# The prelude of a one-layer attention and retention trunk: order of loads, squares and row copies

## The chip, the cores and the metric

The kernel runs on one core of a Trainium2 chip. The time is that of the device for one execution, in microseconds (us); 975.65 us is the median of three runs before the change. A profile of one further execution is the source of all rows.

## What is computed

One layer for 512 positions of width 2048. An adaptive norm turns the row vector c into a shift, a scale and a gate; the normed x goes through one input projection of 7168 columns, then windowed attention and retention, an output projection and a final norm. Only the beginning matters here:

```
mod = silu(c) @ w_ada + b_ada
shift, scale, gate = split(mod, 3)
h = rms_norm(x, g) * (1 + scale) + shift
proj = h @ w_in
```

## The kernel before

**Tiling.** x comes in four tiles of 128 positions (xt0 to xt3, in order outputs xt_110 to xt_113), each 128 by 2048. Products need h with the width on the partitions, so each tile is squared, divided by its root mean square and turned by PE in blocks of 128 columns. The width is cut into 16 blocks k; block 0 is treated apart, so that products with it can start while the other columns of w_ada are still coming. The blocks are grouped as 1, 2, 2, 3, 4, 4.

**The prelude, written out by hand from `warm(WARM[0], psk3)` on.** `squares_a(t)` squares the lower half of a tile on ACT (tile sqa) and `squares(t)` the upper half on DVE (sqd); `factor(t)` makes the factor rsx from both sums, on DVE and then with a power on POOL. `scaled(t, a, b)` multiplies columns a to b by it on DVE. `k0_part(t)` turns block 0 of the tile on PE into psk, or into psk3 for tile 3, and `turned(t, b)` turns one of four groups of further blocks into a PSUM bank psx, which `evacuated(t, b, act)` copies to xT on ACT. The bank comes from a pool of four.

`sums0(b, i)` multiplies one half i of the first shift (b = 0) or scale columns (b = 1) of w_ada, tile raw0, by silu(c) on PE: eight products each, into psa. `sums0_turned()` copies the resulting row on ACT (tile row0) and turns it on PE; `shift_scale0()` adds the small rows and gives sv and av on DVE. The small rows are b_ada and norm_gain, loaded as bg_row, turned on PE and copied as bg on DVE (`turn_rows`). With sv and av, `h0_high` makes the high part of h block 0 (hh0) on ACT, `h0_sum` and `h0_low` the low part (hl0) on DVE; each once for tiles 0 to 2 (A) and once for tile 3 (B). Every product of the projections is made of three with high and low parts (mm3, lines 89 and 91).

`warm(n, ps)` are n products of constants, whose result nobody reads.

**Behind the prelude.** For the next blocks of width, w_ada is loaded in pieces (araw, three buffers). The first piece is multiplied by silu(c) on ACT (line 206), the others are added on DVE (line 210, aacc); the first of them for blocks 1 and 2 is kept behind the last hh0. Its sums go through PE to sv and av, and from there to hh1, hh2 (line 165). Beside it w_in is loaded (raw), split into high (whi, ACT, line 544) and low (wlo, DVE, line 545) and multiplied.

**Order.** Steps inside `pin` keep their order in the program; the others (the ada pieces, the conversions and products, the last scaling of tile 3's upper half) are put among them by a scheduler. Each engine then runs its list strictly in turn, and SP issues its loads strictly in turn too. Loads are issued on three queues: SP's (q1), ACT's (q10) and POOL's (q0). Before the change xt0 is split between ACT and SP, xt1 is on POOL, xt2 and xt3 on ACT, and raw0's four quarters on SP; w_in and araw follow on SP.

The lines that the prediction names: 116 raw0's loads, 123 x's loads, 199 araw's, 565 w_in's; 268 to 270 the small rows; 292 sums0; 299 the row copy; 301 its turn; 304 to 306 shift and scale; 311 and 316 squares; 321 and 325 factor; 329 and 451 scalings; 335 and 343 turns; 354 copies; 364 and 367 h0; 374 warm products. The changed kernel has the same steps one to seven lines away: its sums0 is line 295, its first ada step line 207.

Of the kernel before, what the change touches and what calls it, by code (L numbers as in the profile page):

```python
# [17 lines left out]
P = 128  # L18
D = 2048
S = 512  # L20
# [16 lines left out]
N_PERSIST = 2  # L37
ADA_SPAN = 0.65
TAB_SPAN = 16
WARM = 9, 2, 8, 6, 4  # L40
LAG = 3
RAW, RAW1, WB, LOOK, LEAD, LEAD1, EB, YB = 3, 3, 3, 2, 4, 8, 1, 22
GR = 2
# [6 lines left out]
def trunk_kernel(ctx, tc, x, c, norm_gain, w_ada, b_ada, w_in, w_out, dec_f, dec_b, final_gain, out):  # L50
    nc = tc.nc
    x2, o2 = x[0], out[0]
# [9 lines left out]
    def bank(pool, nm):  # L62
        return pool.tile([P, 512], F32, tag="b", name=nm)
# [49 lines left out]
    xn = [(x3p if t == 3 else xp).tile([P, D], F32, name=f"xt{t}") for t in range(NT)]  # L113

    def load0(q, b, i):
        q.dma_start(
            raw0[b][:, i * 8 : (i + 1) * 8],
            wa[i * 8 * P : (i + 1) * 8 * P, b * D : b * D + P].rearrange("(a p) f -> p a f", p=P),
        )

    nc.gpsimd.dma_start(c_row, c.rearrange("b (k p) -> (b k) p", p=P))
    for q, t, a, b in ((nc.scalar, 0, 0, 1024), (nc.sync, 0, 1024, D), (nc.gpsimd, 1, 0, D), (nc.scalar, 2, 0, D), (nc.scalar, 3, 0, D)):
        q.dma_start(xn[t][:, a:b], x2[t * P : (t + 1) * P, a:b])
    for i in range(2):
        for b in range(2):
            load0(nc.sync, b, i)
    ssx = const.tile([P, NT, 2], F32, name="ssx")
    rsx = const.tile([P, NT], F32, name="rsx")

# [20 lines left out]
    pin = tc.keep_in_program_order  # L150
# [114 lines left out]
    bg = const.tile([P, 48], F32, name="bg")  # L265

    def turn_rows():
        pin(nc.tensor.transpose(ps0[:, 64:112], bg_row, ident[0:48, 0:48]))
        nc.vector.tensor_copy(bg, ps0[:, 64:112])
        nc.vector.tensor_scalar_add(bg[:, 16:32], bg[:, 16:32], 1.0)  # L270

    def silu_c_pe():
        pin(nc.tensor.transpose(ps0[:, 0:NK], c_row, ident[0:NK, 0:NK]))
# [1 line left out]
    def silu_c():  # L275
        pin(nc.scalar.activation(ce, ps0[:, 0:NK], AF.Exp, scale=-1.0))
        pin(nc.vector.tensor_scalar_add(ce, ce, 1.0))
        pin(nc.vector.reciprocal(ce, ce))
        pin(nc.vector.tensor_tensor(ct, ps0[:, 0:NK], ce, op=ALU.mult))
# [3 lines left out]
    ps0 = bank(psA, "ps0")  # L283
# [5 lines left out]
    def sums0(b, i):  # L289
        for a in range(8 * i, 8 * i + 8):  # L290
            pin(
                nc.tensor.matmul(
                    psa[0:1, b * P : (b + 1) * P], ct[:, a : a + 1], raw0[b][:, a, :],
                    start=a + b == 0, stop=a == NK - 1, skip_group_check=True,
                )
            )

    def sums0_turned():
        pin(nc.scalar.copy(row0, psa[0:1, 0 : 2 * P]))
        for b in range(2):  # L300
            pin(nc.tensor.transpose(psa[:, 256 + b : 257 + b], row0[:, b * P : (b + 1) * P], ident[0:1, 0:1]))

    def shift_scale0():
        pin(nc.vector.tensor_tensor(sv[:, 0:1], psa[:, 256:257], bg[:, 0:1], op=ALU.add))
        pin(nc.vector.tensor_tensor(av[:, 0:1], psa[:, 257:258], bg[:, NK : NK + 1], op=ALU.add))
        pin(nc.vector.tensor_tensor(av[:, 0:1], av[:, 0:1], bg[:, 32:33], op=ALU.mult))


    def squares_a(t):
        sa = xp.tile([P, 1024], F32, tag="sqa", name="sqa")  # L310
        marks["sq"] = pin(nc.scalar.activation(sa, xn[t][:, 0:1024], AF.Square, accum_out=ssx[:, t, 0:1]))

    def squares(t):
        sd = aap.tile([P, 1024], F32, tag="aacc", name="sqd")
        v = xn[t][:, 1024:2048]
        pin(nc.vector.tensor_tensor_reduce(sd, v, v, 1.0 / D, EPS, ALU.mult, ALU.add, ssx[:, t, 1:2]))

    def factor(t):
        ms = small.tile([P, 1], F32, tag="ms1", name="ms1", bufs=2)
        pin(  # L320
            nc.vector.scalar_tensor_tensor(
                ms, ssx[:, t, 0:1], 1.0 / D, ssx[:, t, 1:2], op0=ALU.mult, op1=ALU.add
            )
        )
        nc.gpsimd.tensor_tensor(rsx[:, t : t + 1], ms, mhalf[:, 0:1], op=ALU.pow)

    def scaled(t, a, b):
        v = xn[t][:, a:b]
        marks["sc"] = pin(nc.vector.tensor_scalar_mul(v, v, rsx[:, t : t + 1]))
# [3 lines left out]
    def k0_part(t):  # L333
        o = psk3[:, 0:P] if t == 3 else psk[:, t * P : (t + 1) * P]
        pin(nc.tensor.transpose(o, xn[t][:, 0:P], ident))
# [3 lines left out]
    def turned(t, b, late=False):  # L339
        ps = psx[t, b] = bank(psM if late else psP, "psx")  # L340
        for k in range(*BANKS[b]):
            j = k - BANKS[b][0]
            ins = nc.tensor.transpose(ps[:, j * P : (j + 1) * P], xn[t][:, k * P : (k + 1) * P], ident)
            if not late:
                pin(ins)

    def evacuated(t, b, eng, late=False):
        k0, k1 = BANKS[b]
        for i, g in enumerate(groups):
            lo, hi = max(g[0], k0), min(g[-1] + 1, k1)  # L350
            if i and lo < hi:
                dst = xt_tiles[i][:, lo - g[0] : hi - g[0], t * P : (t + 1) * P]
                src = psx[t, b][:, (lo - k0) * P : (hi - k0) * P].rearrange("p (k f) -> p k f", k=hi - lo)
                marks[eng] = eng(dst, src)
                if not late:
                    pin(marks[eng])

    act, dve = nc.scalar.copy, nc.vector.tensor_copy
# [4 lines left out]
    def h0_high(cols, src):  # L363
        marks["hh"] = pin(nc.scalar.activation(hh[0][:, cols], src, AF.Identity, scale=av[:, 0:1], bias=sv[:, 0:1]))

    def h0_sum(cols, src):
        pin(nc.vector.tensor_scalar(tmp0[:, cols], src, av[:, 0:1], sv[:, 0:1], op0=ALU.mult, op1=ALU.add))

    def h0_low(cols):
        marks["hl"] = pin(nc.vector.tensor_tensor(hl[0][:, cols], tmp0[:, cols], f32(hh[0][:, cols]), op=ALU.subtract))  # L370

    def warm(n, ps):
        for _ in range(n):
            pin(nc.tensor.matmul(ps[:, 128:256], ones, ident, start=True, stop=True))

    A, B = slice(0, 3 * P), slice(3 * P, S)
    warm(WARM[0], psk3)
    squares_a(0)
# [5 lines left out]
    silu_c()  # L384
    warm(WARM[1], psk3)
    k0_part(0)
# [2 lines left out]
    scaled(0, 1024, D)  # L389
    turned(0, 2)  # L390
    turned(0, 3)
    for b in range(4):
        evacuated(0, b, act)
    warm(WARM[2], psk3)
    sums0(0, 0)
    turn_rows()
    squares_a(1)
    squares(1)
    factor(1)
    scaled(1, 0, P)  # L400
    scaled(1, P, 1024)
    k0_part(1)
    turned(1, 0)
    turned(1, 1)
    evacuated(1, 0, act)
    evacuated(1, 1, act)
    sums0(1, 0)
    scaled(1, 1024, D)
    turned(1, 2)
    turned(1, 3)  # L410
    sums0(0, 1)
    squares_a(2)
    squares(2)
    factor(2)
    evacuated(1, 2, act)
    evacuated(1, 3, act)
    sums0(1, 1)
    scaled(2, 0, P)
    scaled(2, P, 1024)
    sums0_turned()  # L420
    k0_part(2)
    turned(2, 0)
    turned(2, 1)
    shift_scale0()
    squares_a(3)
    squares(3)
    factor(3)
    h0_sum(A, psk[:, A])
    scaled(3, 0, P)
    scaled(2, 1024, D)  # L430
    evacuated(2, 0, act)
    evacuated(2, 1, act)
    h0_high(A, psk[:, A])
    turned(2, 2)
    warm(WARM[3], ps0)
    k0_part(3)
    warm(WARM[4], ps0)
    h0_low(A)
    marks["conv1"] = [marks["hh"], marks["hl"]]
    h0_high(B, psk3[:, 0:P])  # L440
    h0_sum(B, psk3[:, 0:P])
    h0_low(B)
    turned(2, 3)
    evacuated(2, 2, act)
    evacuated(2, 3, act)
    scaled(3, P, 1024)

    def last_rows(b):
# [868 lines left out]
```

## Time and profile before

| what | value |
|---|---|
| median of three runs | 975.65 us (975.62 to 977.54) |
| profiled execution | 977.17 us |
| its span, first to last instruction | 975.4 us |
| mean granted clock of TensorE | 0.994 |
| first raw0 sums on PE | 15.47 us |
| row copy of the raw0 sums | 29.96 us |
| first ada step (line 206) | 38.90 us |
| first product with h0 | 39.12 us |

The last four are starts, in us from the beginning of the span. PE is TensorE's products, PEld its weight loads, DVE VectorE, ACT ScalarE, POOL GpSimd, SP SyncE. In the timeline a row merges several instructions of one kind (x16), and each fp32 product of 128 columns appears as two. The 1.8 us between span and time lie outside of the instructions.

### The profile page before, as it was taken

The page shows a single profiled execution, that of the slowest core. Times are in us where ns is not written, and L with a number is a line of the kernel's source. Part 1 is how long each engine was busy: PE and PEld are TensorE (multiplying, and loading weights), DVE is VectorE, ACT ScalarE, POOL GpSimd, SP SyncE. Part 2 cuts the span into 40 slices and gives each one's busy share as a digit, 9 for nine tenths or more (in the row PEclk, how much of TensorE's full clock was granted, in tenths as well). Part 3 has the DMA queues.
Part 4 walks back from the last instruction along what each step waited for, and adds up shares of the span by engine and source line. Part 5 has one row for each costly group of instructions (what it writes and reads, how often), then busy time and mean ns, then how long its engine had stood idle before and what let it go on. Part 6 is the DMA issues. An engine that isn't in the chain of part 4 may idle for free.

```text
span 975.4 us, 14424 instructions
## 1 busy us (share of the span) xinstructions
PE 948.7 (97%) x5624; PEld 824.8 (85%) x5624; DVE 614.0 (63%) x1076; ACT 376.3 (39%) x738; POOL 12.8 (1%) x26
## 2 busy tenths in 40 slices
PE   6899899999999999999999999999999999999996
PEld 4787688887988888988998899998899988888896
DVE  3699999957868776664555456745534382535444
ACT  3654425234236554444343232422333372333321
POOL 1000000000000000000000000000000000000001
PEclk9999999999999999999999999999999999999998
DMA  9697879633652122212224625426413148234304
GB/s 330 207 313 241 284 267 314 208 102 111 187 179 80 53 85 65 66 44 87 70 84 149 197 66 184 141 80 202 123 57 95 54 169 283 87 119 140 109 1 173
DMA packets 108947, 141.49 MB, mean 145 GB/s; under 512 B 5656, under 2 KB 78024, under 8 KB 108496
## 3 DMA queue, kind: packets, MB, share of 16 engines
q1 hardware_dynamic: 107056, 134.78, 43.0%
q10 hardware_dynamic: 1584, 4.72, 1.2%
q8 instruction: 44, 0.72, 0.3%
q0 software_dynamic: 240, 1.08, 0.3%
q14 instruction: 23, 0.19, 0.1%
HBM read 136.36 MB, written 4.20 MB: 144 GB/s over the span
## 4 chain that ended last, share of the span: by engine, by line
PE 82%; DVE 7%; DMA 7%; issue 2%; ACT 1%; POOL 0%; SPq 0%; POOLq 0%; DVEq 0%; ACTq 0%
PE pp L91 24%; PE po L91 12%; PE pp L89 12%; PE pw L91 12%; PE po L89 6%; PE pw L89 6%; PE op L91 3%; DMA araw<-in_w_ada_dram 3%; DMA graw<-in_w_ada_dram 2%; PE sp L91 2%; DVE aacc L210 2%; PE op L89 2%; DMA raw<-in_w_ada_dram 1%; PE tp L776 1%; DVE acc L948 1%
## 5 line engine op out<-in xcount | busy, mean ns | idle before, releaser
L544 ACT CAST whi<-raw 128x512 fp32r<-128x512 f32 (+1 forms) x289 | 175.2, 607 | 431.8 <-PE pp L91 197.4
L545 DVE TENSOR_TENSOR wlo<-raw,whi 128x512 fp32r<-128x512 f32 (+1 forms) x289 | 193.6, 671 | 208.5 <-ACT whi L544 204.3
L91 PE MATMUL pp<-wlo,hh 128*128 128x256 f32 x576 | 161.9, 281 | 0.9 <-DVE wlo L545 0.9
L89 PE MATMUL pp<-whi,hh 128*128 128x256 f32 x576 | 162.4, 282 | 0.0
L91 PE MATMUL pp<-whi,hl 128*128 128x256 f32 x576 | 161.5, 280 | 0.0
L89 PEld LDWEIGHTS pp<-whi,hh 128*128 128x128 f32 x576 | 108.5, 188 | 2.5 <-ACT sc L845 1.7
L91 PEld LDWEIGHTS pp<-wlo,hh 128*128 128x128 f32 x576 | 108.5, 188 | 2.1 <-DVE wlo L545 1.3
L91 PEld LDWEIGHTS pp<-whi,hl 128*128 128x128 f32 x576 | 108.5, 188 | 0.0
L89 PE MATMUL pw<-hh,whi 128*128 128x512 f32 x256 | 102.4, 401 | 2.7 <-DVE acc L948 2.0
L89 PE MATMUL pp<-hh,whi 128*128 128x512 f32 x256 | 101.8, 398 | 0.4 <-DVE kl L676 0.4
L91 PE MATMUL pp<-hh,wlo 128*128 128x512 f32 x256 | 101.3, 397 | 0.7 <-DVE wlo L545 0.7
L91 PE MATMUL pw<-hh,wlo 128*128 128x512 f32 x256 | 101.6, 397 | 0.1
L91 PE MATMUL pp<-hl,whi 128*128 128x512 f32 x256 | 101.1, 395 | 0.0
L91 PE MATMUL pw<-hl,whi 128*128 128x512 f32 x256 | 101.0, 395 | 0.0
L91 PE MATMUL po<-wlo,yh 128*128 128x512 f32 (+1 forms) x252 | 92.6, 367 | 0.0
L91 PE MATMUL po<-whi,yl 128*128 128x512 f32 (+1 forms) x252 | 92.5, 367 | 0.0
L89 PE MATMUL po<-whi,yh 128*128 128x512 f32 (+1 forms) x252 | 92.5, 367 | 0.0
L210 DVE SCALAR_TENSOR_TENSOR aacc<-araw,ct,aacc 128x512 f32<-128x512 f32 (+2 forms) x75 | 75.9, 1012 | 7.0 <-ACT aacc L206 3.7
L948 DVE TENSOR_TENSOR acc<-acc,pw 128x512 f32<-128x512 f32 x100 | 66.9, 680 | 8.0 <-PE pw L91 7.6
L1001 DVE SCALAR_TENSOR_TENSOR gacc<-graw,ct,gacc 128x512 f32<-128x512 f32 x60 | 45.0, 749 | 40.2 <-DMA graw<-in_w_ada_dram 39.8
L89 PEld LDWEIGHTS pw<-hh,whi 128*128 128x128 f32 x256 | 48.1, 188 | 17.5 <-DVE acc L948 4.5
L89 PEld LDWEIGHTS pp<-hh,whi 128*128 128x128 f32 x256 | 48.1, 188 | 13.7 <-ACT e L721 0.9
(234 smaller groups left out, 1567.4 us busy)
## 6 DMA issues: line engine op xcount, KB each, us to landing
raw<-in_w_in_dram SPq DMA_DIRECT2D x94, 512.0 KB, 3.6
araw<-in_w_ada_dram SPq DMA_DIRECT2D x48, 512.0 KB, 6.1
graw<-in_w_ada_dram SPq DMA_DIRECT2D x64, 256.0 KB, 2.9
raw<-in_w_out_dram SPq DMA_DIRECT2D x32, 512.0 KB, 3.7
raw<-in_w_in_dram SPq DMA_DIRECT2D x16, 384.0 KB, 3.6
araw<-in_w_ada_dram SPq DMA_DIRECT2D x16, 384.0 KB, 5.2
res<-in_x_dram SPq DMA_DIRECT2D x16, 256.0 KB, 6.2
raw<-in_w_in_dram SPq DMA_DIRECT2D x11, 256.0 KB, 2.8
```

The costliest lines, as they stand in the source:

```text
L89: nc.tensor.matmul(o, lh, rh, start=start, stop=False, skip_group_check=True)
L91: nc.tensor.matmul(o, a, b, start=False, stop=stop and b is (rl if swap else rh), skip_group_check=True)
L210: ins = nc.vector.scalar_tensor_tensor(acc[:, :, :n], rv[:, a], ct[:, kr + a : kr + a + 1], acc[:, :, :n], op0=ALU.mult, op1=ALU.add,)
L544: c1 = nc.scalar.copy(dh, src)
L545: c2 = nc.vector.tensor_tensor(dl, src, f32(dh), op=ALU.subtract)
L776: nc.tensor.transpose(tp_[:, j * P : (j + 1) * P], pt[:, j * P : (j + 1) * P], ident)
L948: nc.vector.tensor_tensor(accs[u][i], accs[u][i], ps[i], op=ALU.add)
L1001: nc.vector.scalar_tensor_tensor(st["acc"], raw, ct[:, kr : kr + 1], st["acc"], op0=ALU.mult, op1=ALU.add)
```

## The change

Loads: xt1 and xt2 go on ACT's queue, xt3 on SP's queue behind the four raw0 quarters; POOL no longer loads x. Squares and factors of tiles 1 and 2 both come before either tile is scaled. The held-back halves of both (`turned(t, 2)`, `turned(t, 3)`) are turned behind the row's turn. `turn_rows` now only turns the rows on PE, ahead of the first sums0; their copy on DVE is the new `rows()`, put behind the scalings of tiles 1 and 2. Tile 3's squares stand ahead of the row copy and of shift and scale. The warm products go from 9, 2, 8, 6, 4 to 9, 2, 4, 4. No arithmetic is changed.

```diff
-WARM = 9, 2, 8, 6, 4
+WARM = 9, 2, 4, 4
...
-    for q, t, a, b in ((nc.scalar, 0, 0, 1024), (nc.sync, 0, 1024, D), (nc.gpsimd, 1, 0, D), (nc.scalar, 2, 0, D), (nc.scalar, 3, 0, D)):
+    for q, t, a, b in ((nc.scalar, 0, 0, 1024), (nc.sync, 0, 1024, D), (nc.scalar, 1, 0, D), (nc.scalar, 2, 0, D)):
...
             load0(nc.sync, b, i)
+    nc.sync.dma_start(xn[3], x2[3 * P : S, :])
...
-        nc.vector.tensor_copy(bg, ps0[:, 64:112])
-        nc.vector.tensor_scalar_add(bg[:, 16:32], bg[:, 16:32], 1.0)
+
+    def rows():
+        pin(nc.vector.tensor_copy(bg, ps0[:, 64:112]))
+        pin(nc.vector.tensor_scalar_add(bg[:, 16:32], bg[:, 16:32], 1.0))
...
+    evacuated(0, 0, act)
+    evacuated(0, 1, act)
+    for t in (1, 2):
+        squares_a(t)
+        squares(t)
+        factor(t)
     warm(WARM[2], psk3)
+    turn_rows()
     sums0(0, 0)
+    evacuated(0, 2, act)
+    evacuated(0, 3, act)
+    for t in (1, 2):
+        scaled(t, 0, P)
+        scaled(t, P, 1024)
+        k0_part(t)
+        turned(t, 0)
+        turned(t, 1)
+        evacuated(t, 0, act)
+        evacuated(t, 1, act)
+        sums0(t % 2, t // 2)
+    sums0(1, 1)
     scaled(1, 1024, D)
+    scaled(2, 1024, D)
+    rows()
     squares_a(3)
     squares(3)
     factor(3)
+    sums0_turned()
+    shift_scale0()
+    for t in (1, 2):
+        turned(t, 2)
+        turned(t, 3)
+    scaled(3, 0, P)
     h0_sum(A, psk[:, A])
     h0_high(A, psk[:, A])
+    k0_part(3)
     warm(WARM[3], ps0)
```

How the engines' lists change is shown at three places. First DVE, from the last scaling of tile 0 to the scale: before the change (xt_111 is tile 1, xt_112 tile 2, xt_113 tile 3; the short rows of the sums are ssx, ms the mean square):

```order
L269 COPY bg<-ps_147 128x48
L270 TENSOR_SCALAR bg<-bg 128x16
L316 ISA sqd,ssx<-xt_111 128x1024
L316 ISA ssx 128x1
L321 SCALAR_TENSOR_TENSOR ms_226<-ssx 128x1
L329 TENSOR_SCALAR xt_111<-xt_111,rsx 128x128
L329 TENSOR_SCALAR xt_111<-xt_111,rsx 128x896
L329 TENSOR_SCALAR xt_111<-xt_111,rsx 128x1024
L316 ISA sqd,ssx<-xt_112 128x1024
L316 ISA ssx 128x1
L321 SCALAR_TENSOR_TENSOR ms_275<-ssx 128x1
```

There the copy of the small rows leads, and tile 2 is squared behind tile 1's scalings. On the same engine after the change, from tile 1's upper half to shift and scale:

```order
L332 TENSOR_SCALAR xt_111<-xt_111,rsx 128x1024
L332 TENSOR_SCALAR xt_112<-xt_112,rsx 128x1024
L272 COPY bg<-ps_147 128x48
L273 TENSOR_SCALAR bg<-bg 128x16
L319 ISA sqd,ssx<-xt_113 128x1024
L319 ISA ssx 128x1
L324 SCALAR_TENSOR_TENSOR ms_292<-ssx 128x1
L445 TENSOR_SCALAR xt_113<-xt_113,rsx 128x1024
L307 TENSOR_TENSOR sv<-psa,bg 128x1
L308 TENSOR_TENSOR av<-psa,bg 128x1
L309 TENSOR_TENSOR av<-av,bg 128x1
```

The squares of tiles 1 and 2 have moved ahead of this piece, the copy of the rows stands behind the last scaling, and the scaling of tile 3's upper half, which the scheduler places, stands ahead of shift and scale; before the change it stood behind the first wlo.

Second ACT, from the row copy to the first ada step, before the change (psk holds block 0 of tiles 0 to 2, psk_148 that of tile 3):

```order
L299 COPY row_149<-psa 1x256
L311 ACTIVATE sqa,ssx<-xt_113 128x1024
L354 COPY xT_93<-psx 128x2x128
L354 COPY xT_94<-psx 128x2x128
L354 COPY xT_95<-psx 128x3x128
L364 ACTIVATE hh_77<-psk,sv,av 128x384
L544 CAST whi<-raw 128x512
L364 ACTIVATE hh_77<-psk_148,sv,av 128x128
L354 COPY xT_96<-psx 128x4x128
L206 ACTIVATE aacc<-araw,ct 128x2x256
```

And the same stretch of ACT after it:

```order
L314 ACTIVATE sqa,ssx<-xt_113 128x1024
L302 COPY row_149<-psa 1x256
L367 ACTIVATE hh_77<-psk,sv,av 128x384
L538 CAST whi<-raw 128x512
L367 ACTIVATE hh_77<-psk_148,sv,av 128x128
L357 COPY xT_96<-psx 128x4x128
L357 COPY xT_97<-psx 128x4x128
L357 COPY xT_96<-psx 128x4x128
L357 COPY xT_97<-psx 128x4x128
L207 ACTIVATE aacc<-araw,ct 128x2x256
```

Tile 3's squares now lead the row copy, and four copies instead of one stand between the last hh and the ada step.

Third PE, from the warm products behind tile 0 to the row's turn, before the change (raw_108 holds the shift columns, raw_109 the scale columns):

```order
L374 MATMUL psk_148<-ident,ones 128x128 x8
L292 MATMUL psa<-raw_108,ct 1x128 x8
L268 MATMUL ps_147<-ident,bg_row 128x48
L335 MATMUL psk<-ident,xt_111 128x128
L343 MATMUL psx<-ident,xt_111 128x128 x7
L292 MATMUL psa<-raw_109,ct 1x128 x8
L343 MATMUL psx<-ident,xt_111 128x128 x8
L292 MATMUL psa<-raw_108,ct 1x128 x8
L292 MATMUL psa<-raw_109,ct 1x128 x8
L301 MATMUL psa<-ident,row_149 128x1 x2
```

And PE's same stretch after it, with the turns that now follow:

```order
L377 MATMUL psk_148<-ident,ones 128x128 x4
L269 MATMUL ps_147<-ident,bg_row 128x48
L295 MATMUL psa<-raw_108,ct 1x128 x8
L338 MATMUL psk<-ident,xt_111 128x128
L346 MATMUL psx<-ident,xt_111 128x128 x7
L295 MATMUL psa<-raw_109,ct 1x128 x8
L338 MATMUL psk<-ident,xt_112 128x128
L346 MATMUL psx<-ident,xt_112 128x128 x7
L295 MATMUL psa<-raw_108,ct 1x128 x8
L295 MATMUL psa<-raw_109,ct 1x128 x8
L304 MATMUL psa<-ident,row_149 128x1 x2
L346 MATMUL psx<-ident,xt_111 128x128 x8
```

The turn of the small rows now leads the first sums, tile 2's first seven blocks stand between the sums, and the second half of tile 1 (and of tile 2 behind it) has moved behind the row's turn.

Further on, at the ada step of the next group but one, ACT has the step ahead of all four short sums (junk) instead of between two and two; from there on the three lists of ACT, DVE and SP soon are the same as before.

More of the change, by code (lines that the diff above doesn't have):

```diff
@@ L391, in trunk_kernel @@
     turned(0, 3)
-    for b in range(4):
-        evacuated(0, b, act)
+    evacuated(0, 0, act)
[4 more added lines that the diff above has]
+        factor(t)
     warm(WARM[2], psk3)
+    turn_rows()
     sums0(0, 0)
[L396 to L407, printed above, removed]
-    scaled(1, 1024, D)
[L409 to L424, printed above, removed]
+    evacuated(0, 2, act)
[10 more added lines that the diff above has]
+    sums0(1, 1)
+    scaled(1, 1024, D)
+    scaled(2, 1024, D)
+    rows()
     squares_a(3)
@@ L427, in trunk_kernel @@
     factor(3)
+    sums0_turned()
[4 more added lines that the diff above has]
+    scaled(3, 0, P)
     h0_sum(A, psk[:, A])
[L429 to L432, printed above, removed]
     h0_high(A, psk[:, A])
-    turned(2, 2)
+    k0_part(3)
     warm(WARM[3], ps0)
-    k0_part(3)
-    warm(WARM[4], ps0)
     h0_low(A)
@@ L442, in trunk_kernel @@
     h0_low(B)
-    turned(2, 3)
-    evacuated(2, 2, act)
-    evacuated(2, 3, act)
+    for t in (1, 2):
+        evacuated(t, 2, act)
+        evacuated(t, 3, act)
     scaled(3, P, 1024)
```

## The prediction

> **What bounds the kernel now.** The page's first part comes first: who is busy over the whole span.
>
> ```profile
> PE 948.7 (97%) x5624; PEld 824.8 (85%) x5624; DVE 614.0 (63%) x1076; ACT 376.3 (39%) x738; POOL 12.8 (1%) x26
> ```
>
> 97% is a mean over stages, and says nothing of the prelude. Next the chain of work in order of time (start, duration, what); three of its longest pieces are transfers:
>
> ```profile
> 1.19 14.23 DMA raw<-in_w_ada_dram
> ...
> 69.52 7.67 DMA araw<-in_w_ada_dram
> ...
> 158.44 6.46 DMA araw<-in_w_ada_dram
> ```
>
> So the end hangs on loads from the first microsecond on, and on araw loads as late as 158. Then the timeline of the prelude (start, duration, engine, line, operation, in brackets the idle time before it with its releaser):
>
> ```profile
> 15.47 1.91 PE L292 MATMUL psa<-raw,ct 128*1 128x128 f32 x16 [2.35 <-DMA raw<-in_w_ada_dram]
> 17.60 0.21 DVE L269 COPY bg<-ps 128x48 f32<-128x48 f32 x1 [7.42 <-PE ps L268]
> 17.93 1.22 DVE L316 CUSTOM_DVE_ANT_0 sqd<-xt 128x1024 f32<-128x1024 f32 x1
> ...
> 19.50 0.55 POOL L325 TENSOR_TENSOR rsx<-ms,mhalf 128x1 f32<-128x1 f32 x1 [11.47 <-DVE ms L321]
> ...
> 25.24 1.10 PE L343 MATMUL psx<-ident,xt 128*128 128x128 f32 x8
> 26.27 3.65 PE L292 MATMUL psa<-raw,ct 128*1 128x128 f32 x32
> 29.96 0.36 ACT L299 COPY row<-psa 1x256 f32<-1x256 f32 x1 [2.95 <-PE psa L292]
> 30.76 0.16 DVE L304 TENSOR_TENSOR sv<-psa,bg 128x1 f32<-128x1 f32 x1 [4.62 <-PE psa L301]
> 33.21 0.67 ACT L364 ACTIVATE hh<-psk,sv,av 128x384 fp32r<-128x384 f32 x1 [0.79 <-DVE ht L367]
> 33.78 0.61 ACT L544 CAST whi<-raw 128x512 fp32r<-128x512 f32 x1
> 38.08 0.46 ACT L364 ACTIVATE hh<-psk,sv,av 128x128 fp32r<-128x128 f32 x1 [3.69 <-PE psk L335]
> 38.43 0.58 ACT L354 COPY xT<-psx 128x512 f32<-128x512 f32 x1
> 38.90 0.73 ACT L206 ACTIVATE aacc<-araw,ct 128x512 f32<-128x512 f32 x1
> 39.12 0.48 PE L89 MATMUL pw<-hh,whi 128*128 128x512 f32 x1
> ```
>
> The reader is to see one serial line. The first w_ada columns (raw0) land at 15.4. Only behind their sums does PE turn bg_row; DVE, which has stood at the bg copy for 7.42 us, then squares tile 1, though the tile had been there (ACT squared its half at 12.61, below). Then come factor, scaling and transposes, tile after tile; the first ada piece (L206) starts at 38.90 and the first product with h0 at 39.12. The same windows show what the DMA engines do (the last two columns: DMA share, GB/s) and the granted clock (the column before them):
>
> ```profile
> 5.00:14.20 9.20, 7.29 (x49) 6.34 (x48) 3.45 (x9) 4.59 (x10) 0.56 (x1) 1.00 1.03 400
> 14.20:20.50 6.30, 2.16 (x18) 1.47 (x18) 2.09 (x7) 0.00 (x0) 0.55 (x1) 1.00 1.20 298
> 20.50:24.30 3.80, 3.44 (x17) 2.38 (x18) 2.27 (x4) 2.06 (x5) 0.00 (x0) 0.55 1.04 390
> 24.30:34.00 9.70, 6.92 (x60) 5.08 (x57) 4.07 (x12) 4.42 (x12) 1.10 (x2) 1.00 1.02 326
> 34.00:44.00 10.00, 9.66 (x52) 8.79 (x53) 7.25 (x14) 6.31 (x15) 0.00 (x0) 0.83 0.14 40
> 44.00:62.00 18.00, 17.26 (x101) 14.45 (x100) 16.84 (x32) 13.39 (x26) 0.00 (x0) 1.00 0.96 315
> ```
>
> The DMA engines are full to 34, idle for 86% of the next 10 us (8.6 us), full again from 44. So whatever starts the ada pieces earlier finds the engines free. Up to the araw load of 158.44 the chain alternates between DVE, such loads and PE; each load is issued when DVE frees its buffer, so an earlier start is passed on.
>
> **Part 1: the loads.** x's tile 1 leaves POOL for ACT's queue, tile 3 goes from ACT to SP's queue behind raw0. DMA queues in the window from 6 to 14 us (packets, MB, share):
>
> ```profile
> q10 hardware_dynamic: 263, 1.90, 58.7%
> q0 software_dynamic: 228, 1.08, 33.1%
> q1 hardware_dynamic: 422, 0.22, 9.2%
> ```
>
> q10 is ACT's, q0 POOL's, q1 SP's. SP's raw0 rows are 512 bytes, those of x 8 KB; packets go out at comparable counts, so raw0 gets 0.22 of 3.2 MB and moves at its own pace (298 GB/s) only when x is through. Three tiles of x stand before it now, two after the change: 1.05 MB at 400 GB/s is 2.6 us. First raw0 quarter usable: 15.47 - 2.6 = **12.85**; each further quarter (0.524 MB at 298) 1.76 later, the fourth at 18.1. x's tile 3 follows: 18.1 + 2.6 = 20.7. All this is estimated from these rows. The bytes before the w_in loads are the same, so those loads start where they did.
>
> ```profile
> 1.19 14.10 SPq L116 DMA_DIRECT2D raw<-in_w_ada_dram  x4
> 15.33 4.11 SPq L565 DMA_DIRECT2D raw<-in_w_in_dram  x6
> ...
> 1.93 0.56 POOL L123 DMA_DIRECT2D xt<-in_x_dram  x1
> ```
>
> SP's sequencer stands in raw0's issues until 15.3; these end earlier as raw0 drains earlier, and the added issue (0.46, half of the 0.92 for two at 46.69 below) stands in front of transfers that cannot move before 20.7: nothing. POOL loses an issue of 0.56; the warm-up products start that much earlier and then wait for c_row: nothing.
>
> [...]
>
> **Part 2: the squares ahead.** Durations of the moved steps:
>
> ```profile
> 12.61 1.06 ACT L311 ACTIVATE sqa<-xt 128x1024 f32<-128x1024 f32 x1 [0.60 <-DMA xt<-in_x_dram]
> ...
> 35.18 0.75 DVE L451 TENSOR_SCALAR xt<-xt,rsx 128x1024 f32<-128x1024 f32 x1
> ...
> 11.17 1.95 PE L374 MATMUL psk<-ident,ones 128*128 128x128 f32 x16
> ```
>
> ACT: two copies of tile 0 to 10.7, squares of tile 1 to 12.0, of tile 2 to 13.2 (1.06 each, with the short read of the sum behind it 1.25). DVE squares in step (1.22 each), POOL's powers take 0.55; tile 1 is scaled from about 13.6, tile 2 to 15.4. All of it lies beside the wait for raw0, which PE needs to 12.85 + 1.83 = 14.7 in any case. The two late copies of tile 0 (1.1 us of ACT) lie there too. If the cover goes (x later by 1 us), the margin of 1 us is used up and each further us costs one.
>
> PE then has no wait left: four sums of 3.65 / 2 = 1.83 are 7.3, two tiles' k0 part and seven transposes 2 x 1.10 = 2.2; 12.85 + 9.5 = 22.35, against 29.92 now. The second and fourth quarters of raw0 are there when PE arrives (14.6 for 15.8, 18.1 for 20.5).
>
> **Part 3: rows late, tile 3, h0.** The bg copy (0.21 and 0.17) now lies in DVE's free time at 17: nothing. The row copy on ACT has tile 3's squares ahead of it: 20.7 + 1.25 = 22.0, so it still starts at 22.4; by the rows 29.96 and 30.76 the shift can start 0.80 later, 23.2. On DVE tile 3's squares, factor and, as the order shows, the 0.75 us scaling of its upper half stand ahead: 22.0 + 0.2 + 0.75 (power with its gaps) + 0.75 = 23.7. That is late next. Shift and scale, three small steps of 0.16, end at 24.1, high h0 and the cast take ACT to 25.4. PE's 16 held-back transposes end at 23.2 + 2.2 = 25.4, tile 3's k0 part at 25.7, four warm products (0.98) at **26.7**, where the first product starts: 12.4 before 39.12. ACT: high part of tile 3 to 26.2, then four copies (now one) of 0.58 less some overlap to 28.4, then L206.
> Its load: w_in 1.70 MB (3328 columns of 128 rows, 4 bytes) at 390 from 20.7 is 25.1, one araw pair 1.05 MB at 326 is 28.3, landing perhaps 0.7 later. I take **28.7**, 10.2 before 38.90 (between 9.9 and 10.5). DVE is full in 44:62 (16.84 of 18), so this, not PE's 12.4, is what counts.
>
> **Part 4: what comes through.**
>
> ```profile
> 46.69 0.92 SPq L199 DMA_DIRECT2D araw<-in_w_ada_dram  x2
> ...
> 54.09 0.72 ACT L206 ACTIVATE aacc<-araw,ct 128x512 f32<-128x512 f32 x1 [1.02 <-DMA araw<-in_w_ada_dram]
> ...
> 74.64 0.28 ACT L243 ACTIVATE junk<-psm 128x128 f32<-128x128 f32 x1 [1.07 <-PE psm L238]
> ...
> 77.28 0.94 ACT L206 ACTIVATE aacc<-araw,ct 128x768 f32<-128x768 f32 x1 [2.01 <-DMA araw<-in_w_ada_dram]
> ```
>
> The load that ends a wait at 54.0 has, counted from 34, 3.14 MB to go (two w_in loads of 0.26, araw 1.05, w_in 0.52, its own 1.05): 9.6 us at 326 is 43.6, landing 44.3, a shift of 9.7 instead of 10.2. At 74.6 two sums (0.6 us) are now behind the ada piece that waits for its load: up to -0.6, and as one of DVE's casts stands one add earlier there (0.75), the load may come sooner: between -0.6 and +0.7; I take 0, the middle. From about 125 on the three orders are the same, so nothing more is gained or lost. Sum: **9.7 us**; 977.17 of the profiled execution becomes 967.5. That execution is 1.5 over the median of the runs; on the median: 975.65 - 9.7 = 966.0.
>
> **Rivals.**
> Raw0 not earlier: if raw0 gets its pace no sooner, PE starts at 15.47, all moves by 2.6, gain 7.1: 968.6. For it: SP's queue also carries tile 3. Against it: 298 GB/s begins only where x ends.
>
> A throttled clock. These rows show it:
>
> ```profile
> 20.90:24.30 3.40, 3.18 (x16) 2.31 (x17) 1.87 (x4) 2.06 (x5) 0.00 (x0) 0.53 1.03 389
> 34.55:38.00 3.45, 3.45 (x19) 3.45 (x19) 1.38 (x3) 0.00 (x0) 0.00 (x0) 0.54 0.25 77
> ```
>
> Each follows a stretch in which PE had little. With 10 warm products fewer, the 16 held-back transposes could run at half clock: 2.2 us more, gain 7.5: 968.2. Against it: PE is busy without a gap from 12.85.
> [...]
>
> The stream caps it: if the loads of 44:62 are bound by bytes throughout, the gain is the 8.6 us of idle DMA: 967.1.
>
> PE's own 12.4 comes through where araw waits shrink: 963.3.
>
> Slower: tile 3's load. ACT's row copy and DVE's shift stand behind its squares. If SP's queue did not keep its order and tile 3 landed with the last of the batch, at 34, the row copy would start at 35.25, L206 6.0 later (28.4 - 22.4) at 41.25, 2.35 behind now: 978.0. It decides from a landing at 31.65 on, and is measurable from 33.6. Against it: the rate goes from 298 to 390 at 20.5, so w_in followed raw0 in order.
>
> It does nothing: all comes back in the waits at 54 and 77, if the araw buffers and not the start set them: about 975.6. Against it: 8.6 us of idle DMA and an issue (46.69) that waits for DVE.
>
> **How the numbers follow.** Forecast 966.0, 0.62; PE's gain 0.07; cap 0.07; raw0 not earlier 0.09; clock 0.06; nothing 0.04; slower 0.05. Without the last two cases all lie between 963.3 and 968.6; raw0 and clock together would give 970.8. Range 963.2 to 969.6. Faster by over 0.2% (about what a measurement of this kernel can tell from no change, 1.95 us) 0.91, within 0.04, slower 0.05.
>
> **What would show it.** Right: first L295 at 12.9, the row copy at 22.4, L207 between 28 and 29.3, first product near 26.7, no half clock after 13, DMA share near 1 from 5 to 45, the second L207 near 44.4. Wrong: row copy later than 24 (tile 3 or raw0), a clock of 0.5 between 20 and 30, or a wait for araw at 44 to 70 that is longer than 2 us, which would give the gain back.

## The result, and the profile after

| | before | after |
|---|---|---|
| median of four runs each | 975.69 us (975.62 to 977.54) | 965.07 us (963.96 to 966.97) |
| profiled execution (its span) | 977.17 us (975.4) | 963.96 us (962.1) |
| mean granted clock of TensorE | 0.994 | 0.998 |

The ratio is 0.9889, with a 95% interval from 0.9867 to 0.9911: a gain of 10.8 us (8.7 to 13.0); between the medians it is 10.6. The forecast was 966.0 and its range 963.2 to 969.6. The first part of the page of after hardly differs from that of before:

```profile
PE 945.0 (98%) x5604; PEld 822.1 (85%) x5604; DVE 614.4 (64%) x1076; ACT 376.0 (39%) x738; POOL 13.6 (1%) x25
```

TensorE has 3.7 us less to do, and 20 products fewer in the record: the ten warm products that were dropped, each shown as two. What the change did is seen in the prelude. This is the timeline of after (start, duration, engine, line, operation, in brackets the idle time before it with its releaser):

```profile
13.38 1.91 PE L295 MATMUL psa<-raw,ct 128*1 128x128 f32 x16
...
13.98 3.16 DVE L332 TENSOR_SCALAR xt<-xt,rsx 128x128 f32<-128x128 f32 x6 [0.17 <-POOL rsx L328]
...
17.06 0.20 DVE L272 COPY bg<-ps 128x48 f32<-128x48 f32 x1
...
19.10 3.65 PE L295 MATMUL psa<-raw,ct 128*1 128x128 f32 x32
22.36 1.23 DVE L319 CUSTOM_DVE_ANT_0 sqd<-xt 128x1024 f32<-128x1024 f32 x1 [4.89 <-DMA xt<-in_x_dram]
...
23.48 0.34 ACT L302 COPY row<-psa 1x256 f32<-1x256 f32 x1
...
25.19 0.15 DVE L307 TENSOR_TENSOR sv<-psa,bg 128x1 f32<-128x1 f32 x1
...
27.50 0.46 ACT L367 ACTIVATE hh<-psk,sv,av 128x128 fp32r<-128x128 f32 x1
...
27.85 2.04 ACT L357 COPY xT<-psx 128x512 f32<-128x512 f32 x4
28.01 0.73 PE L89 MATMUL pw<-hh,whi 128*128 128x512 f32 x2 [0.94 <-ACT hh L367]
...
29.75 0.76 ACT L207 ACTIVATE aacc<-araw,ct 128x512 f32<-128x512 f32 x1
```

The serial line that could be read in the profile of before is gone. VectorE scales tile 1 at 13.98, while PE takes its first sums; the copy of the small rows (17.06) comes without a wait in front of it, where it had 7.42 us; PE runs to the last sums at 19.10 without a stop of more than 0.3. One long wait is left on DVE, 4.89 us before 22.36, and it ends on a transfer: x's tile 3. The first ada step is at 29.75, 9.15 earlier than before. The windows of after (busy time of PE, PEld, DVE, ACT, POOL, then granted clock, DMA share, GB/s) answer to those of before:

```profile
14.20:20.50 6.30, 6.30 (x55) 4.68 (x54) 3.16 (x8) 2.21 (x7) 0.70 (x1) 1.00 1.13 349
20.50:24.30 3.80, 2.69 (x25) 1.93 (x23) 1.39 (x3) 1.40 (x3) 0.36 (x1) 1.00 1.03 387
24.30:34.00 9.70, 7.87 (x47) 6.12 (x46) 7.66 (x17) 7.58 (x17) 0.19 (x1) 1.00 1.08 346
34.00:44.00 10.00, 10.00 (x56) 8.56 (x55) 9.56 (x16) 9.72 (x21) 0.00 (x0) 1.00 1.01 324
44.00:62.00 18.00, 17.92 (x116) 15.80 (x115) 16.98 (x31) 7.51 (x13) 0.00 (x0) 1.00 0.98 326
```

The stretch 34 to 44, in which the DMA engines had a share of 0.14, now has 1.01; PE's 2.16 of 6.30 us (14.2 to 20.5) have become 6.30; and the granted clock is 1.00 in each row, where it was 0.55 and 0.83 in two. The ada steps further on, in the timeline of ACT:

```profile
44.37 0.72 ACT L207 ACTIVATE aacc<-araw,ct 128x512 f32<-128x512 f32 x1 [0.18 <-DMA araw<-in_w_ada_dram]
...
65.76 0.93 ACT L207 ACTIVATE aacc<-araw,ct 128x768 f32<-128x768 f32 x1
```

They were at 54.09 and 77.28, so the shift is 9.72 and then 11.52. At the fourth and fifth it is 11.47 (112.33 to 100.86) and 10.34 (154.94 to 144.60).

### The profile page after: what moved, and what is told of

Read it like the earlier page. It is cut to its first block, busy times and chain, and to the rows that moved or that the text cites. A ratio compares the mean times of both kernels' runs of the same rounds, so it can differ in the third digit from the quotient of the medians.

```text
span 962.1 us, 14387 instructions
## 1 busy us (share of the span) xinstructions
PE 945.0 (98%) x5604; PEld 822.1 (85%) x5604; DVE 614.4 (64%) x1076; ACT 376.0 (39%) x738; POOL 13.6 (1%) x25
## 4 chain that ended last, share of the span: by engine, by line
PE 87%; DVE 5%; DMA 4%; issue 2%; SPq 1%; ACT 1%; POOL 0%; POOLq 0%; DVEq 0%; ACTq 0%
PE pp L91 24%; PE pw L91 14%; PE pp L89 12%; PE po L91 12%; PE pw L89 7%; PE po L89 6%; PE op L91 3%; PE sp L91 2%; DMA graw<-in_w_ada_dram 2%; PE op L89 2%; PE tp L770 1%; DVE aacc L211 1%; SPq L116 1%; PE sp L89 1%; DMA xt<-in_x_dram 1%
```

## The experiments

Ten runs followed; e0 is the changed kernel once more. "Gain" is one minus the ratio to the kernel before, times the median of that kernel measured beside it (975.98 for e1 to e4, 976.6 for e0, e6, e9 and e10, 976.79 for e12 and e13), with the 95% interval. The three ada steps are starts on ACT in one profiled execution each; between the changed kernel and e0 they differ by 0.2 to 0.7, less than the whole time scatters, and so they place what a kernel's time alone leaves open.

| kernel | ada steps at | median | gain |
|---|---|---|---|
| before | 38.90, 54.09, 77.28 | 975.69 | |
| after | 29.75, 44.37, 65.76 | 965.07 | 10.8 (8.7 to 13.0) |
| e0, after again | 29.91, 44.60, 66.48 | 965.47 | 11.0 (9.4 to 12.7) |
| e1, before + new loads | 36.52, 52.01, 74.14 | 974.58 | 2.3 (1.1 to 3.5) |
| e2, after - new loads | 30.45, 45.25, 66.89 | 967.41 | 9.3 (7.7 to 10.8) |
| e3, after, rows early | 34.24, 49.00, 71.47 | 970.5 | 6.1 (4.7 to 7.5) |
| e9, e3 + warm products | 33.27, 48.47, 69.33 | 968.75 | 7.8 (6.2 to 9.6) |
| e4, after, squares in turn | 29.39, 44.12, 65.60 | 964.92 | 11.0 (9.4 to 12.8) |
| e10, before + 18 and 18 warm | 39.03, 55.00, 77.29 | 975.66 | 0.8 (-0.4 to 1.9) |
| e13, before + 9 and 10 warm | 35.84, 51.46, 74.32 | 973.61 | 3.6 (2.3 to 4.9) |
| e6, after, tile 3 earlier | 29.48, 44.29, 65.70 | 965.97 | 10.8 (9.2 to 12.5) |
| e12, e6 + araw earlier | 28.38, 44.22, 65.05 | 965.23 | 12.0 (10.5 to 13.6) |

### The loads: e1 and e2

e1 is the kernel before with the change's three lines on the loads (x's tile 1 on ACT's queue, tile 3 behind raw0) and nothing else; e2 is the changed kernel without them:

```diff
-    for q, t, a, b in ((nc.scalar, 0, 0, 1024), (nc.sync, 0, 1024, D), (nc.scalar, 1, 0, D), (nc.scalar, 2, 0, D)):
+    for q, t, a, b in ((nc.scalar, 0, 0, 1024), (nc.sync, 0, 1024, D), (nc.gpsimd, 1, 0, D), (nc.scalar, 2, 0, D), (nc.scalar, 3, 0, D)):
...
-    nc.sync.dma_start(xn[3], x2[3 * P : S, :])
```

> The kernel before with the new placement of the loads alone (tiles 1 and 2 of x on ACT's queue, tile 3 on SP's behind raw0); the order of all engines stays that of before. My theory: raw0's first quarter is usable at 12.9 instead of 15.47 and everything behind it moves by that much, gain 2.6, about 973.1 us; the row copy near 27.4. Rival, the loads are the whole effect: a gain of 8 or more, below 968. Rival, the order is the whole effect: 975.7.

> The changed kernel with the old placement of the loads (tile 1 on POOL's queue, tiles 2 and 3 on ACT's); the order of all engines stays that of the changed kernel. Theory of tile 3: in the changed kernel PE reached raw0 at 13.38 and the shift waited for tile 3 (usable at 22.4), so the loads bought only part of their 2.6 us; here PE starts at 15.4, the row copy comes at 24.9 instead of 23.48, the shift at 25.7 instead of 25.19, and the loss is 0.5 to 1.2 us: 965.6 to 966.3. Rival of the prediction: the loss is the full 2.6, about 967.7. Rival, the loads are the whole effect: above 973.

From the timeline of e1:

```profile
12.98 1.91 PE L293 MATMUL psa<-raw,ct 128*1 128x128 f32 x16
...
36.52 0.73 ACT L207 ACTIVATE aacc<-araw,ct 128x512 f32<-128x512 f32 x1
```

And from that of e2:

```profile
15.67 1.91 PE L294 MATMUL psa<-raw,ct 128*1 128x128 f32 x16 [1.01 <-DMA raw<-in_w_ada_dram]
...
25.89 0.16 DVE L306 TENSOR_TENSOR sv<-psa,bg 128x1 f32<-128x1 f32 x1 [1.03 <-PE psa L303]
...
30.45 0.77 ACT L206 ACTIVATE aacc<-araw,ct 128x512 f32<-128x512 f32 x1
```

In the old order the first sums come 2.49 earlier (15.47 to 12.98) and the first ada step 2.38 earlier: the loads are worth what the first term of the prediction said, as long as everything hangs on raw0. In the new order the sums come 2.3 later without the new loads, but the first ada step only 0.70 and the second 0.88: tile 3, which comes with the rest of x there, keeps nobody waiting (shift waits for PE), and most of the 2.3 is made good behind it. On the time e2 missed: it is 2.3 above the changed kernel, over the 0.5 to 1.2 that were expected and near the rival's full 2.6. But its ada steps do not show that rival: the third is 1.13 later and the fifth 0.28 (144.88 for 144.60). The intervals of the two gains overlap, so the rest is not shown to come from the loads, and where it arises is open.

### The early rows, and the clock behind them: e3 and e9

e3 puts the small rows' turn and copy back ahead of the squares, as before the change; e9 is e3 with 24 warm products in the hole that this leaves on PE:

```diff
+    warm(WARM[2], psk3)
+    sums0(0, 0)
+    turn_rows()
+    rows()
     for t in (1, 2):
         squares_a(t)
         squares(t)
         factor(t)
-    warm(WARM[2], psk3)
-    turn_rows()
-    sums0(0, 0)
...
-    rows()
```

```diff
     turn_rows()
+    warm(24, psk3)
     rows()
```

> The changed kernel with the small rows turned behind the first sums and copied on DVE ahead of the squares of tile 1, as before the change; the rest as changed. My theory: DVE stands at the copy until the first raw0 sums are done (15.6), squares both tiles only then, tile 1's first block is turned at about 19.2 instead of 15.2, the row copy comes at about 26.7 instead of 23.48; loss 2.4 to 3.1 us, 967.5 to 968.2. Rival, the copy is hidden wherever it stands: 965.1.

> The kernel with the small rows early (e3) and 24 more products of constants on PE behind the turn of the rows, where PE stood idle for 3.78 us and the granted clock then was 0.5 from 17 to 24. Theory of the clock: of e3's loss of 5.4 us, 2.0 to 2.4 are the half clock (sums of 3.17 instead of 1.91, turns of 1.73 instead of 0.93); with PE kept busy the row copy comes at 26.7 instead of 28.87 and the time is 2 to 2.4 below e3's, about 968.2. Rival, the whole loss is DVE's wait: no change against e3, 970.5.

The timeline of e3:

```profile
14.96 0.21 DVE L272 COPY bg<-ps 128x48 f32<-128x48 f32 x1 [4.92 <-PE ps L269]
...
19.39 1.73 PE L346 MATMUL psx<-ident,xt 128*128 128x128 f32 x7 [0.21 <-DVE xt L332]
...
21.05 3.17 PE L295 MATMUL psa<-raw,ct 128*1 128x128 f32 x16
...
34.24 0.77 ACT L207 ACTIVATE aacc<-araw,ct 128x512 f32<-128x512 f32 x1
```

Its windows (busy PE, granted clock, DMA share, GB/s):

```profile
12.00:17.10 5.10, 2.18 (x18) 0.98 1.21 290
17.10:23.90 6.80, 4.98 (x23) 0.52 1.04 395
```

And the timeline of e9:

```profile
14.92 5.62 PE L377 MATMUL psk<-ident,ones 128*128 128x128 f32 x48
...
20.49 0.93 PE L346 MATMUL psx<-ident,xt 128*128 128x128 f32 x7
21.35 1.91 PE L295 MATMUL psa<-raw,ct 128*1 128x128 f32 x16
...
33.27 0.76 ACT L207 ACTIVATE aacc<-araw,ct 128x512 f32<-128x512 f32 x1
```

With the rows early, VectorE stands 4.92 us at their copy again, with the squares of two tiles behind it, and the first ada step comes 4.49 later than in the changed kernel; the time is about 5 us longer (5.4 between the medians, 4.7 between the gains), where 2.4 to 3.1 had been expected. Most of the difference is the clock. PE has 2.18 us of work in 5.1, and in the next 6.8 us the granted clock is 0.52: the seven turns take 1.73 instead of 0.93, the sums 3.17 instead of 1.91, 2.06 us for these two rows. e9 keeps the stall (4.99) and takes away the half clock. Its warm products ran to 20.4, past the 18.71 at which tile 1's block began in e3, so that the turns start 1.10 later (20.49 for 19.39); still the row copy (27.90 for 28.87) and the first ada step are 0.97 earlier than in e3. That is under half of the 2.2 expected for the row copy. The gain is 1.7 larger, where 2 to 2.4 had been expected, and the intervals overlap: it is the rows that show the effect, not the time alone. So the early rows cost twice: by the stall itself, and by the clock that falls behind PE's idle time.

### What the clock cost the kernel before: e10 and e13

Both fill the two idle stretches of PE in the kernel before with warm products, and move nothing else; e10 has 18 in each, e13 9 and 10:

```diff
     turn_rows()
+    warm(9, psk3)
     squares_a(1)
...
     h0_high(A, psk[:, A])
+    warm(10, psk3)
     turned(2, 2)
```

> The kernel before with 18 more products of constants in each of PE's two idle stretches (17.6 to 20.4 and 31.7 to 34.3), behind which the granted clock was 0.5 for 3.4 us each; nothing else moves. Theory of the clock: the first half-clock stretch cost 1.4 us (turns of 1.73 for 0.93, sums of 2.53 for 1.91), the second 2.2 (twelve and eight warm halves at 0.21 instead of 0.13, turns of 1.09 for 0.55); the first ada step comes 3.6 earlier, near 35.3, and the time is 972 to 972.7. Rival, the clock sets nothing there: 975.7 to 976.

> The kernel before with 9 warm products in its first idle stretch of PE (17.5 to 20.4) and 10 in its second (31.65 to 34.3), half as many as in e10, where 18 took 5.1 and 4.2 us and pushed tile 1's block from 20.43 to 23.03. Nothing else moved. Theory A (the half clock after idle stretches costs the kernel before some 1.5 to 2.5 us in the chain up to the first ada group, as e9 against e3 shows for the early row copy): 18 halves at 0.142 are 2.6 us and fit in the first gap, so tile 1's block stays at 20.4 to 20.8, turns of 8 tiles take about 0.93 to 1.1 instead of 1.73, sums 1.9 instead of 2.53, and the row copy comes 1 to 2 us earlier: 973.5 to 974.8 against 976 for before. Rival B (the clock's share is hidden behind DVE and ACT in the order of before, and only the new order exposes it): the granted clock is 1.0 in both stretches and the time stays within 0.5 of before.

Ahead of them the kernel before, in its timeline:

```profile
20.43 0.33 PE L335 MATMUL psk<-ident,xt 128*128 128x128 f32 x1 [2.87 <-DVE xt L329]
21.12 1.73 PE L343 MATMUL psx<-ident,xt 128*128 128x128 f32 x7 [0.36 <-DVE xt L329]
22.78 2.53 PE L292 MATMUL psa<-raw,ct 128*1 128x128 f32 x16
```

The timeline of e10:

```profile
18.09 5.10 PE L374 MATMUL psk<-ident,ones 128*128 128x128 f32 x36
23.03 0.27 PE L335 MATMUL psk<-ident,xt 128*128 128x128 f32 x1
```

That of e13:

```profile
17.45 2.27 PE L374 MATMUL psk<-ident,ones 128*128 128x128 f32 x18
20.39 0.33 PE L335 MATMUL psk<-ident,xt 128*128 128x128 f32 x1 [0.66 <-DVE xt L329]
21.07 0.95 PE L343 MATMUL psx<-ident,xt 128*128 128x128 f32 x7 [0.36 <-DVE xt L329]
21.96 1.91 PE L292 MATMUL psa<-raw,ct 128*1 128x128 f32 x16
...
28.51 0.36 ACT L299 COPY row<-psa 1x256 f32<-1x256 f32 x1 [2.95 <-PE psa L292]
...
35.84 0.73 ACT L206 ACTIVATE aacc<-araw,ct 128x512 f32<-128x512 f32 x1
```

And the windows of e13 in which the kernel before had part of its time at half clock, with means of 0.56 and 0.64 (to PE's, PEld's, DVE's, ACT's and POOL's busy time, clock, DMA share, GB/s):

```profile
20.40:24.30 3.90, 3.54 (x29) 2.63 (x30) 2.49 (x5) 2.07 (x5) 0.22 (x1) 1.00 1.04 391
...
34.30:39.00 4.70, 4.70 (x34) 4.20 (x33) 3.65 (x8) 3.98 (x10) 0.00 (x0) 1.00 0.21 62
```

e10 missed: its 36 half products took 5.10 us in a hole of 2.9, put tile 1's block from 20.43 to 23.03, and so gave back what the clock gained. Part of the 5.10 is a half clock of its own: behind the wait for raw0 the granted clock was 0.50 from 16.40 to 19.80. So its time says nothing of the clock's price. Half as many fit (2.27 us): tile 1's block stays at 20.39, the turns take 0.95 instead of 1.73, the sums 1.91 instead of 2.53, the row copy comes 1.45 earlier, and with the second hole filled the first ada step comes 3.06 earlier. The gain is 3.6 (2.3 to 4.9), and the median of 973.61 lies within the 973.5 to 974.8 expected. The granted clock over whole executions agrees: 0.996 to 0.998 in the six of e13, 0.990 to 0.994 in the eleven of the kernel before that ran beside them. The rival, that DVE and ACT hide the clock in the old order, falls. So some 3 us of the 10 that the change wins can be had in the kernel before with 19 warm products and no other step.

### The squares ahead: e4

```diff
-    for t in (1, 2):
-        squares_a(t)
-        squares(t)
-        factor(t)
...
     for t in (1, 2):
+        squares_a(t)
+        squares(t)
+        factor(t)
         scaled(t, 0, P)
```

> The changed kernel with the squares of each tile directly ahead of its own scaling (tile 2's squares behind tile 1's turn and copies); the rest as changed. Theory of tile 3: tile 2's first block is turned at about 19.4 instead of 18.1 and the row copy comes at about 24.1 instead of 23.48, but the shift waits for tile 3's squares and scaling on DVE anyway (25.2); loss 0 to 0.6 us, 965.1 to 965.7. Rival, squares ahead of scalings carry the change: a loss of 3 us or more, above 968.

The timeline of e4:

```profile
14.57 1.22 DVE L319 CUSTOM_DVE_ANT_0 sqd<-xt 128x1024 f32<-128x1024 f32 x1
...
19.44 0.96 PE L346 MATMUL psx<-ident,xt 128*128 128x128 f32 x7 [0.36 <-DVE xt L332]
...
24.02 0.36 ACT L302 COPY row<-psa 1x256 f32<-1x256 f32 x1 [1.84 <-PE psa L295]
...
29.39 0.77 ACT L207 ACTIVATE aacc<-araw,ct 128x512 f32<-128x512 f32 x1
```

Tile 2 is squared behind tile 1's scalings, PE's turns of tile 2 come at 19.44 instead of 18.25, and the row copy waits for PE and not for tile 3. It starts 0.54 after the changed kernel's, though PE had begun its sums 0.54 sooner (12.84 for 13.38). The first ada step comes no later (29.39 against 29.75), since tile 3's squares, which began at 22.36 there, had begun at 20.85 here and were through by then; that tile 3 was there so early is scatter of its load (see below). The time is that of the changed kernel (964.92 against 965.07 and 965.47). The squares of two tiles ahead of the scalings, one of the steps of the change, are worth nothing that can be measured: by e3, what counts is that they aren't behind the copy of the small rows.

### What bounds the prelude now: e0, e6 and e12

e0 is the changed kernel once more. e6 loads tile 3 between raw0's second and third quarter; e12 is e6 with the first pair of araw loads ahead of five of the six first w_in loads:

```diff
     for i in range(2):
         for b in range(2):
             load0(nc.sync, b, i)
-    nc.sync.dma_start(xn[3], x2[3 * P : S, :])
+        if i == 0:
+            nc.sync.dma_start(xn[3], x2[3 * P : S, :])
```

```diff
         if ci == 0:
+            items[0]["load"]()
+            agenda[fed + LAG].pop(0)()
             for it in items:
                 it["load"]()
```

> The changed kernel once more, as the control of this call. Expected 964 to 966.5 us as before. In the first profile tile 3 was usable at 22.4, in the one with squares in turn at 20.9 at the latest; if that is scatter of the transfer, it lies anywhere between 20.8 and 22.4 here, with the row copy between 22.8 and 23.5.

> The changed kernel with tile 3's load on SP's queue between the second and the third quarter of raw0 instead of behind the fourth; nothing else moves. Theory of tile 3: its squares are done before the sums end, DVE's shift follows the row copy by 0.8 us; raw0's last two quarters come 2.6 later (usable at 19.2 and 21 to 22) and PE needs them at 19.1 and 20.9, so the row copy stays at 22.8 to 24 and the shift comes at 23.6 to 24.8 instead of 25.19: gain 0.3 to 1.2 us. Rival, raw0's end is what counts: a loss of up to 1.3 us.

> The changed kernel with two loads moved: tile 3 between the second and the third raw0 quarter (as in e6), and the first pair of w_ada tiles of the first ada group (1 MB) ahead of five of the six first loads of w_in (1.6 MB). Same bytes by the time the fourth pair of that group has landed, same work, same order on PE, ACT and DVE but for names. Theory A (from 11 to 65 us the DMA engines are full, and the first ada group ends when its fourth pair has landed): the first product of the group at L207 comes up to 1.2 us earlier than in e6 (28.2 instead of 29.48, the wait for araw gone, behind the four ACT copies), but the second L207 stays at 44.0 to 44.6, and the time stays where the changed kernel is: 965.0 to 966.2. Rival B (what was late in e6 was the first pair alone): second L207 1.2 earlier, near 43.1, and the time 0.8 to 1.5 below the changed kernel, about 964.2. Rival C (the five loads of w_in that now land some 3 us later keep PE waiting between 28 and 38): idle of PE there of 1 us and more, released by ACT whi, and a time above 966.5.

The timeline of e0:

```profile
21.55 1.23 DVE L319 CUSTOM_DVE_ANT_0 sqd<-xt 128x1024 f32<-128x1024 f32 x1 [3.68 <-DMA xt<-in_x_dram]
...
29.91 0.72 ACT L207 ACTIVATE aacc<-araw,ct 128x512 f32<-128x512 f32 x1 [0.82 <-DMA araw<-in_w_ada_dram]
```

The timeline of e6:

```profile
17.20 1.22 DVE L320 CUSTOM_DVE_ANT_0 sqd<-xt 128x1024 f32<-128x1024 f32 x1 [0.23 <-DMA xt<-in_x_dram]
...
25.84 0.46 ACT L368 ACTIVATE hh<-psk,sv,av 128x128 fp32r<-128x128 f32 x1
...
29.48 0.72 ACT L208 ACTIVATE aacc<-araw,ct 128x512 f32<-128x512 f32 x1 [1.24 <-DMA araw<-in_w_ada_dram]
```

The timeline of e12:

```profile
28.38 0.77 ACT L208 ACTIVATE aacc<-araw,ct 128x512 f32<-128x512 f32 x1
...
44.22 0.72 ACT L208 ACTIVATE aacc<-araw,ct 128x512 f32<-128x512 f32 x1 [1.40 <-DMA araw<-in_w_ada_dram]
```

e6 takes tile 3 off the path: it is there at 17.20, and h0 is complete 1.66 us earlier (the last hh at 25.84 instead of 27.50; in e0, where tile 3 came sooner, it was at 26.70). The first ada step gains 0.27 only, since it now waits for its first pair of loads, and the time gains nothing, against the 0.3 to 1.2 expected. e12 takes away that wait as well: the first step starts 1.37 earlier than in the changed kernel. And the second still starts at 44.22, behind a wait of 1.40 for its own load. In five profiles (the changed kernel, e0, e4, e6, e12) the first ada step lies between 28.38 and 29.91, and the second between 44.12 and 44.60. The bytes up to that load are the same in all of them, and the DMA engines have a share of 0.98 to 1.13 from 14 to 62 in the rows of the changed kernel. So it is the stream of bytes that sets the second step now, and none of the orders tried in front of it has moved it. Neither kernel is measurably better than the changed one.

## Why the prediction was right

**The bound.** "One serial line" and "the DMA engines are idle for 86% of the next 10 us" were the two readings it rested on, and both hold: undoing the step that breaks the line (e3) loses about half of the gain, and the idle stretch has gone to a share of 1.01.

**The loads.** First quarter usable at 12.85: the sums start at 13.38, behind PE's own earlier work, and without a wait for the load; where PE was free sooner (e3, e4, e6, e9), at 12.83 to 12.91 and behind the load. The 2.6 us were right for raw0, by e1 as well, and the rival "raw0 not earlier" falls. Moving two tiles of x between queues moved the first raw0 sums by 2.5 us (15.47 to 12.98); which of the two moves did it, e1 does not tell, since it makes both. The rival's price, that without this term all would come 2.6 later, is not borne out: in e2 the first two ada steps are late by 0.70 and 0.88. The issue of tile 3's load, put at 0.46, took 1.73 (from 12.71), and it cost nothing all the same: w_in's issues began at 14.49 instead of 15.33.

**PE without a wait.** To 22.35 by the sum, 22.75 by the row 19.10 + 3.65. The sum took full-clock durations for all of it, and from the first sums on these are the ones that came. Ahead of them PE was slower: tile 0's fifteen turns took 3.46 us from 8.89, where the kernel before had 0.98 and 1.09 for them, and so the sums began at 13.38. (In e0 the last thirteen of the same turns took 2.91, and the mean granted clock of its first 20 us was 0.91; in the changed kernel's profile the clock column reads 1.00 there, and the durations are the better guide.) The prediction also counted as waits what was partly the clock: e13 shows that 1.45 us of what it booked under "PE then has no wait left" is the half clock, and 1.61 more of what it booked behind the row copy. The rival "a throttled clock" did not happen: the 16 held-back transposes took 1.97 us at a clock of 1.00.

**Tile 3** is the term that was mis-sized. "x's tile 3 follows: 18.1 + 2.6 = 20.7": it was used from 22.36, 1.66 later. Row copy (23.48 for 22.4), shift (25.19 for 23.7) and the first product (28.01 for 26.7) are late by 1.1 to 1.5 with it. In other executions with the same order of loads its squares began at 21.55 (e0), 22.16 (e9) and, with no wait for it, at 20.85 (e4); the landing scatters by 1.5 us, and why is open. It sets h0, and by e6 not the time.

**The first ada step.** 28.7 was forecast, with 28 to 29.3 as the sign of being right, and 29.75 came: a shift of 9.15 and not 10.2. Two causes lie close together: the four copies on ACT, late with h0, keep it to 29.75 in this profile, and the load itself lands near 29.5 to 29.9 where that can be seen (e0, e6).

**What comes through.** Second ada step at 44.4: it came at 44.37. This term was reckoned by bytes, and so was blind to the error in the one ahead of it. That it fits to 0.1 is in part luck: the sum holds 0.7 for the landing, for which no row was given, and in the five profiles the step lies anywhere from 44.12 to 44.60. Behind it the forecast took 0 between -0.6 and +0.7. The two profiled executions show 1.8 more at the third step and 13.2 at the end; but the first of the two is 1.5 above its median and the second 1.1 below, and the third step of the kernel before waited 2.01 for its load, where e1 and e10, with the same order there, waited 0.95 and 1.10. At the fifth step 10.34 is left of the 11.52, and e0 has the same (144.63). Between the medians the gain is 10.6, 0.9 more than the 9.7 forecast, which lies within the interval. Whether the rows of the third step bring part of that 0.9 was not tried.

**The rivals.** "The stream caps it" (8.6) lies at the edge of the interval (8.7 to 13.0) and close to the forecast (9.7); the time alone hardly tells them apart, but the second ada step moved by 9.72. e6 and e12 show that its mechanism holds for the two further steps that were tried. "PE's own 12.4" is inside the interval too, but it is not what came through: the first product moved by 11.1, and the second ada step by 9.7. Tile 3 as a cause of loss needed a landing at 31.65; its latest was 22.36.

## What to carry to other kernels

Where an engine that runs in order stands at a copy of little weight, look at what is queued behind it: here a row of 0.21 us, behind a wait of 7.42, kept the squares of the next tile waiting, and with them TensorE, whose clock then fell to 0.55 (20.50 to 24.30). When a serial stretch has been shortened until the DMA engines are full, count the bytes up to the next wait: that sum was right to 0.1 us (in part by luck) where the sum over the steps was off by one, and it showed here when further moves of steps stopped paying. An idle stretch of TensorE on a path cost its own length here, and in some cases a half clock after it (2.87 us idle, then 0.50 from 20.67 to 24.08); fillers kept the clock up (1.00 in e13 and e9) but took their own time: 2.3 us in a hole of 2.9 kept the gain (e13), 5.1 in 2.9 gave all of it back (e10), and 5.6 in 3.8 about half (e9).

## What the runs showed of the hardware

In the kernel before, the granted clock was 0.50 from 20.67 to 24.08 and from 34.32 to 37.73, 3.41 us each; in the 3.41 us ahead of them PE had been busy for 0.55 and 0.77 us. In e3 it was 0.52 from 17.10 to 23.90, behind 2.18 us of work in 5.10; e1 and e0 have the lower clock in means only, 0.96 up to 20 us and 0.87 from 20 to 40 in e1, 0.91 up to 20 in e0. Not every idle stretch was followed by it: behind a wait of 2.35 us ahead of 15.47 the clock of the kernel before stayed at 1.00 (14.20 to 20.50), while behind one of 2.33 us ahead of 15.34 that of e10 was 0.50 (16.40 to 19.80). What decides between the two, no run shows. With more work in the idle stretches the clock stayed up: in e13 PE was busy for 2.74 of the 3.40 us from 17.00 and for 2.26 of the 2.70 us from 31.60 (0.56 and 0.08 in the kernel before), and the clock was 1.00 in the two windows behind them, where it had been 0.56 and 0.64. What had not been expected is the price on a serial path: 3.06 us at the first ada step of the kernel before, in a kernel whose mean clock is 0.994.

The 16 held-back transposes of after, 1.97 us from 24.08, ran at a clock of 1.00. In e0 thirteen of tile 0's turns were slow, 2.91 us from 9.69 (0.22 each, where those 16 took 0.12 each), with nothing else on PE; the eight halves of warm products behind them took 1.06 us, as they did in after at a clock of 1.00. So the full pace came back there behind a stretch of 2.9 us that held transposes only.

A load of 1 MB that follows others on one queue became usable over a spread of 1.5 us (20.85 at the latest in e4, 22.36 in after) in kernels with the same order of loads.
